# A mixed trunk step on one core: another order of the background work in layer 0

## The chip, the core and the metric

The kernel runs on one core of a Trainium2 chip. A core has TensorE (PE in the profile; its weight loads are PEld), VectorE (DVE), ScalarE (ACT), GpSimd (POOL) and SyncE (SP), which issues most DMAs. Each engine takes its instructions in the order of the program and stops at one whose inputs or buffer aren't there. The metric is device time in microseconds (us). Of the kernel before there are three runs: median 2731.98, from 2730.38 to 2736.82.

## The reference

One step of a decoder trunk of two layers for 1024 prompt tokens and 64 sampled tokens (8 requests of 8), D = 1024. Both layers have the same frame:

```python
h = x
for layer in range(DEPTH):
    hn = rms_norm(h, norm_mix_g[layer])
    # layer 0: conformer_sb_mixer, layer 1: shortconv_pool_mixer
    h = h + mix
    h = h + swiglu(rms_norm(h, norm_ffn_g[layer]), w_ffn_in[layer], w_ffn_out[layer])
y = rms_norm(h, norm_final_g)
```

The change concerns the mixer of layer 0:

```python
proj = hn @ w_in
a_val, a_gate, q, k, v = jnp.split(proj, ...)              # 512 columns each
glu = a_val * jax.nn.sigmoid(a_gate)
a = causal_depthwise_conv(concat([conv_prev, glu]), conv_w) + conv_b   # 31 taps
a = jax.nn.silu(layer_norm(a, ln_g, ln_b))
b = stick_breaking_attention(q, k_all, v_all, sb_bias, q_pos, k_pos)   # 8 heads x 64
out = concat([a, b]) @ w_out
```

and in the attention, for each head and each block of 128 queries,

```python
z = (q @ k.T) * scale + bias
log_1m = jnp.where(mask, jax.nn.log_sigmoid(-z), 0.0)
after = lax.cumsum(log_1m, axis=3, reverse=True) - log_1m
wgt = jnp.exp(jnp.where(mask, jax.nn.log_sigmoid(z) + after, -jnp.inf))
o = wgt @ v
```

The weight of a key is thus sigmoid(z) times the product of sigmoid(-z) over all later keys, and the kernel computes it so, with a running product in place of the sum of logarithms. For the sampled tokens, k and v of 1024 past positions come from a paged cache.

## The kernel before, in words

**Layout and groups.** Activations lie transposed: 128 channels on the partitions, tokens along the free axis, 8 tiles for D. Tokens are in two groups in layer 0: GA is tokens 0 to 511 (one block of 512 columns), GB is tokens 512 to 1087, prompt and samples (two blocks of 288). Layer 1 takes all tokens as GT.

**The foreground.** The matmuls of the projections are the foreground. Each operand is split into a high part in fp32r and the remainder, and `mm3` (L170) makes three passes of high and low parts. Weights stream in pieces of 128x1024: SP loads a piece into `stage`, ACT copies it to the high part of `hl` (L152), POOL subtracts for the low part (L153); `hl` has three buffers. A *block* is one output of 128 channels: 8 tiles by 3 passes by the group's column blocks, 24 matmuls for GA and 48 for GB. DVE then takes the result out of `acc`, times the tokens' norm factors `rr` (`scaled`, L226), or adds it to `hb` (L230). The order of the program is: projection of GA, projection of GB, output projection and FFN of GA, the same of GB, then layer 1.

**Slots and flows.** Within a block, ahead of its tiles 2, 4 and 6, and once behind it, the foreground calls a slot, and a slot runs one piece of the background: up to the next `yield` of the generator at the head of `flow`. So every `yield` in a generator moves all its later work by one slot, a quarter of a block. What a piece issues stands in the engines' queues between the foreground's instructions. Two flows matter:

- `flow_ab` runs during the projection of GB, and begins in that of GA: `conv_a` (the convolution of GA), `conv_norm(GA)` (layer norm and silu), `attention(GA)`. `drain` at the end of GB's projection issues whatever is left of it.
- `flow_c` runs during GA's output projection and FFN: `attention(GB)`, then `conv_b` (the convolution of GB) and `sample` (attention of the sampled tokens on the paged cache) in turn, then `conv_norm(GB)`.

**The norm of the projection.** The projection starts before the factors of the RMS norm are known: the first two blocks' results are kept unscaled in `raw`. `in_proj(GA, ...)` starts at output 2. In the middle of that block `norm_a` sums the squares over the partitions (PE L194, four matmuls of one column), takes the inverse root on ACT and DVE and lays it on a diagonal (`tmp`, DVE L209); behind the block `norm_b` spreads it over the partitions with one matmul by `ones` (PE L218) and copies it to `rr`. The evacuations `evs` of this and of the raw blocks follow. This block runs no slots. `slot_a` counts its calls: it feeds GB's tokens in (`feed`), then GB's own norm, and each call also runs a piece of the background, which starts to work once GB's factors are there (`phase["start"]`).

**conv_a.** For each of four tiles of 128 channels ACT writes the gated values, with 30 columns ahead, into `ext` (L641; one buffer). DVE adds 26 taps into `acc` in PSUM (L653 the first, L655 the others), two to a slot; the 5 others are products on ACT, which POOL adds into `a2` (L647). L660 joins `acc` and `a2` into `a`, which lies in `aall` (shown as hb in the profile).

**conv_norm.** Sums over channels on POOL and PE, squares on ACT, added on POOL into `ss` (L187), which L194 waits for; then for each tile the product with the factors (POOL), the sigmoid of the affine value (ACT), the affine value itself (DVE L744) and the product of both (POOL).

**attention.** A unit is a head and a block of 128 queries, 32 units to a group, four to a head. `s1` computes scores into `z` in PSUM (PE L796) and two sigmoids of it into `q` and `be` (ACT L801); `s2` makes on DVE the running product over `q` by scans and multiplies it into `be` (L815); `s3` turns `be` by PE (L825) into `m` and copies it to `wt` (ACT L826); `s4` multiplies by the values, `o` (PE L834), which ACT copies out (L835). `operands` sets a head's keys and queries up (`kt`, `qa`, `qz`, L773 to L779). In a step u of the loop these run for different units: s4 of u-3, s2 of u-1, for GB a yield, s1 of u, s3 of u-2, then a yield. `zp` and `op_` hold one buffer of z and of o each, `wt` one, `q` two, `be` three.

Of the kernel before, what the change touches and what calls it, by code (L numbers as in the profile page):

```python
# [8 lines left out]
F = mybir.dt.float32  # L9
FR = mybir.dt.float32r  # L10
I32 = mybir.dt.int32
AF = mybir.ActivationFunctionType
OP = mybir.AluOpType
# [45 lines left out]
def trunk_kernel(ctx, tc, x_prompt, x_sample, cache_k, cache_v, state_conformer, state_shortconv, state_pool,  # L59
# [36 lines left out]
    def pc(c):  # L96
        return par[:, c:c + 1]
# [123 lines left out]
    def norm_b(g, ps, dg):  # L221
        spread(g, ps, dg, 1.0)
# [406 lines left out]
    OFF = 5  # L629

    def conv_a(ep, cp):
        g = GA
        for c in range(4):
            while (g.c0, c) not in glu_done:
                yield None
            a = aall[:, c, g.cs]
            ext = ep.tile([128, CW - 1 + HALF], F, name="ext")
            a2 = ep.tile([128, HALF], F, name="a2")
            acc = cp.tile([128, 512], F, name="cacc")
            pool.memset(ext[:, 0:CW - 1], 0.0)  # L640
            act.activation(ext[:, CW - 1:], a, AF.Copy)  # L641

            def otap(j):
                t = a2 if j == 0 else ep.tile([128, HALF], F, name="tapb", bufs=2)
                act.activation(t, ext[:, j:j + HALF], AF.Copy, scale=pc(CONVW + j * 4 + c))
                if j:
                    pool.tensor_tensor(a2, a2, t, op=OP.add)  # L647

            yield 1
            for j in range(OFF, CW):  # L650
                w, i = pc(CONVW + j * 4 + c), ext[:, j:j + HALF]
                if j == OFF:
                    dve.tensor_scalar(acc, i, w, pc(CONVB + c), op0=OP.mult, op1=OP.add)  # L653
                else:
                    dve.scalar_tensor_tensor(acc, i, w, acc, op0=OP.mult, op1=OP.add)  # L655
                if j % 4 == 1 and j // 4 <= OFF:
                    otap(j // 4 - 1)
                if (j - OFF) % 2 == 1:
                    yield 1
            dve.tensor_tensor(a, acc, a2, op=OP.add)  # L660

    def conv_b(ep, cp):
        stc = {}
# [50 lines left out]
    def conv_norm(g):  # L714
# [22 lines left out]
        for c in range(5):  # L737
            if c < 4:
                pool.tensor_tensor(aall[:, c, cs], aall[:, c, cs], rr[:, cs], op=OP.mult)
            if c:  # L740
                y = aall[:, c - 1, cs]
                t = tmp()
                act.activation(t[:, :n], y, AF.Sigmoid, scale=pc(LNG + c - 1), bias=pc(LNB + c - 1))
                dve.tensor_scalar(y, y, pc(LNG + c - 1), pc(LNB + c - 1), op0=OP.mult, op1=OP.add)  # L744
                pool.tensor_tensor(y, y, t[:, :n], op=OP.mult)
            yield 1
            if g is GB:
                yield 1


    def attention(g):
# [3 lines left out]
        with ExitStack() as es_:  # L755
# [31 lines left out]
            def s1(u):  # L787
# [8 lines left out]
                        pe.matmul(z[:, b, :nm], q[:, (i - i0) * 128:(i - i0) * 128 + 128], kt_[h][:, b * w:b * w + nm],  # L796
                                  start=s == 0, stop=s == 1)
                q = qt[u] = pa.tile([128, NKEY], F, name="q2", bufs=2)
                be = bt[u] = pa.tile([128, NKEY], F, name="be", bufs=3)
                for o, sgn, bi in ((q, -0.125, 1), (be, 0.125, 0)):  # L800
                    act.activation(o[:, :n].rearrange("p (b w) -> p b w", b=nb), z[:, 0:nb, :w], AF.Sigmoid,  # L801
                                   scale=sgn, bias=bh[:, bi, h:h + 1])
# [35 lines left out]
            operands(0)  # L838
            while small:
                small.pop(0)()  # L840
            yield 1
            for u in range(len(units) + 3):
                if u >= 3:
                    s4(u - 3)
                if 1 <= u < len(units) + 1:
                    s2(u - 1)
                if g is GB:
                    yield 1
                if u < len(units):
# [3 lines left out]
                    if r == 2 and h < 7:  # L853
                        load_v(h + 1)
                    s1(u)
                if 2 <= u < len(units) + 2:
                    s3(u - 2)
                for _ in range(2):
                    if small:
                        small.pop(0)()  # L860
# [215 lines left out]
    def in_proj(g, x, first, slot):  # L1076
        evs = [(ev_av, ev_ag, ev_q, ev_k, ev_v)[j](g, c) for j, c in EVEN]
        for i in range(first, len(evs)):
            h = w_next()
            a = accs()  # L1080
            if i == first and first:
                box = {}
                block(g, a, h, x, mid=lambda: box.setdefault("d", norm_a(g, ms, D)))
                norm_b(g, ms, box["d"])
                evs[i](a)
                for j in range(2):
                    evs[j](None, raw[j])
# [376 lines left out]
```

## Time and profile before

| | us |
|---|---|
| median of three runs | 2731.98 |
| the profiled execution | 2730.78 |
| its span, first to last instruction | 2729.0 |
| PE busy in the span | 2612.9 |
| DVE, POOL, ACT busy | 1224.5, 1035.5, 860.4 |

The mean granted clock of TensorE is 0.985. The stretch that the change concerns ends at about 1120 us. The projection of GA fills it up to 166, that of GB up to 370, GA's output projection and FFN take the rest: the attention of GB up to 606, the second convolution with the sampled tokens up to 1020, the norm behind it up to 1120. Here, for each stretch, are its length, the busy time of PE, of its weight loads, of DVE, ACT and POOL (with the number of instructions), the granted clock, the busy share of the DMA engines and their GB/s:

```profile
160.00:240.00 80.00, 69.43 (x486) 67.51 (x486) 39.91 (x57) 28.96 (x41) 55.73 (x37) 0.93 0.27 75
240.00:370.00 130.00, 126.35 (x857) 111.20 (x857) 85.91 (x122) 84.03 (x188) 32.07 (x46) 0.97 0.28 78
370.00:606.00 236.00, 214.89 (x1216) 173.88 (x1217) 179.76 (x164) 144.95 (x230) 88.29 (x71) 0.99 0.20 56
1020.00:1120.00 100.00, 83.99 (x337) 64.91 (x337) 38.09 (x54) 32.41 (x45) 67.45 (x39) 0.91 0.31 98
```

A line of a waits view reads "engine, tile, line <- engine, tile, line: us in total, times, longest": the instructions of the left line stood idle until the right one was done. A line of a timeline reads start, duration, engine, line, operation, output<-inputs, shape; "[5.14 <-DVE tmp L209]" is the idle time just ahead and what ended it, and "x8" stands for so many in a row.

### The profile page before, as it was taken

To read this page: it belongs to the slowest core of one execution; us is meant where nothing else is said; L and a number is where in the kernel's file an instruction comes from. 1 tells how busy PE (TensorE), PEld (TensorE's weight loads), DVE (VectorE), ACT (ScalarE), POOL (GpSimd) and SP (SyncE) were. 2 spreads that over 40 slices of the span, in tenths; PEclk is the share of its full clock that TensorE was granted. 3 is DMA by queue.
4 is the path that set the end of the run, shared out by engine and by line. 5 is a ranking of instruction groups with operands and counts; after the bars stand their busy time and mean duration, and the time that the engine had idled before them with its cause. 6 is when DMAs were issued, how large, how long until landed. Compare 5 with 4: busy or idle time off the path is not lost. (4 is left out here: it accounts for less than half of the span.)

```text
span 2729.0 us, 37771 instructions
## 1 busy us (share of the span) xinstructions
PE 2612.9 (96%) x15423; PEld 2370.5 (87%) x15423; DVE 1224.5 (45%) x1738; ACT 860.4 (32%) x1318; POOL 1035.5 (38%) x589
## 2 busy tenths in 40 slices
PE   7988999899999998899999999999999999999997
PEld 5787877777766656899999989999999999999997
DVE  3775767768777652332222243342222222222226
ACT  4435656653343323242222232123211111111112
POOL 5655233433333327454444452223322222222222
PEclk9999999999999998999999999999999999999999
DMA  6332241124445432422222231131111111111111
GB/s 199 108 102 62 60 114 47 54 64 147 133 132 148 125 116 62 151 78 86 79 85 85 86 99 39 39 100 51 46 44 47 47 40 46 47 43 43 47 39 66
DMA packets 293381, 218.75 MB, mean 80 GB/s; under 512 B 21506, under 2 KB 248962, under 8 KB 293193
## 3 DMA queue, kind: packets, MB, share of 16 engines
q1 hardware_dynamic: 293176, 216.33, 26.6%
q8 instruction: 122, 2.00, 0.3%
q14 instruction: 51, 0.41, 0.0%
q10 hardware_dynamic: 32, 0.01, 0.0%
HBM read 198.09 MB, written 18.69 MB: 79 GB/s over the span
## 5 line engine op out<-in xcount | busy, mean ns | idle before, releaser
L153 POOL TENSOR_TENSOR hl<-stage,hl 128x1024 fp32r<-128x1024 f32 x278 | 683.5, 2461 | 1204.6 <-ACT hl L152 790.0
L170 PE MATMUL acc<-x1t,hl 128*128 128x364 f32 (+1 forms) x4896 | 824.1, 330 | 7.1 <-DVE hb L230 6.4
L170 PEld LDWEIGHTS acc<-x1t,hl 128*128 128x128 f32 x4896 | 817.1, 189 | 9.2 <-ACT x1t L304 6.7
L170 PE MATMUL acc<-x,hl 128*128 128x288 f32 (+1 forms) x4704 | 809.3, 326 | 8.8 <-POOL hl L153 3.2
L170 PEld LDWEIGHTS acc<-x,hl 128*128 128x128 f32 x4704 | 688.2, 189 | 88.8 <-issue 36.0
L170 PE MATMUL acc<-hid,hl 128*128 128x364 f32 (+2 forms) x3024 | 534.5, 335 | 19.9 <-DVE hb L230 15.5
L170 PEld LDWEIGHTS acc<-hid,hl 128*128 128x128 f32 x3024 | 482.2, 191 | 58.5 <-DVE hb L230 20.9
L152 ACT ACTIVATE hl<-stage 128x1024 fp32r<-128x1024 f32 x278 | 291.9, 1053 | 584.3 <-PE acc L170 303.1
L226 DVE TENSOR_TENSOR tmp<-acc,rr 128x728 f32<-128x728 f32 (+2 forms) x230 | 160.8, 721 | 698.1 <-PE acc L170 697.2
L230 DVE TENSOR_TENSOR hb<-acc,hb 128x728 f32<-128x728 f32 (+2 forms) x368 | 255.6, 720 | 280.3 <-PE acc L170 278.9
L176 DVE TENSOR_TENSOR hid<-tmp,hid 128x512 fp32r<-128x512 f32 (+2 forms) x66 | 60.8, 921 | 200.7 <-ACT hid L175 200.7
L187 POOL TENSOR_TENSOR ss<-ss,tmp 128x512 f32<-128x512 f32 (+2 forms) x55 | 97.6, 1774 | 92.9 <-ACT tmp L186 91.9
L175 ACT ACTIVATE hid<-tmp 128x512 fp32r<-128x512 f32 (+2 forms) x66 | 53.5, 810 | 238.4 <-POOL tmp L378 238.3
L378 POOL TENSOR_TENSOR tmp<-tmp 128x512 f32<-128x512 f32 (+2 forms) x66 | 117.0, 1772 | 28.0 <-ACT tmp L366 27.9
L170 PE MATMUL acc<-x1a,hl 128*128 128x512 f32 x480 | 123.0, 410 | 3.4 <-POOL hl L153 2.3
L366 ACT ACTIVATE tmp<-tmp 128x576 f32<-128x576 f32 (+1 forms) x44 | 39.6, 900 | 256.1 <-DVE tmp L226 256.1
L170 PEld LDWEIGHTS acc<-x1a,hl 128*128 128x128 f32 x480 | 90.7, 193 | 27.2 <-POOL hl L153 3.8
L834 PE MATMUL o<-wt,vrow 128*64 128x128 f32 x576 | 78.1, 282 | 16.6 <-ACT wt L826 16.6
L834 PEld LDWEIGHTS o<-wt,vrow 128*64 128x64 f32 x576 | 62.5, 139 | 35.5 <-ACT wt L826 30.3
L688 DVE SCALAR_TENSOR_TENSOR cacc<-ext,par,cacc 128x512 f32<-128x512 f32 x120 | 90.1, 750 | 2.3
L364 POOL TENSOR_TENSOR tmp<-tmp 128x512 f32<-128x512 f32 x22 | 32.4, 1471 | 135.9 <-ACT tmp L363 125.1
L813 DVE TENSOR_TENSOR_SCAN q<-q,ones 128x384 f32<-128x384 f32 (+6 forms) x56 | 77.7, 1388 | 2.0
(222 smaller groups left out, 1898.0 us busy)
## 6 DMA issues: line engine op xcount, KB each, us to landing
stage<-in_w_ffn_in_dram SPq DMA_DIRECT2D x132, 512.0 KB
stage<-in_w_ffn_out_dram SPq DMA_DIRECT2D x66, 512.0 KB
stage<-in_w_in_even_dram SPq DMA_DIRECT2D x40, 512.0 KB
kst<-in_cache_k_dram SPq DMA_DIRECT2D x64, 256.0 KB
vst<-in_cache_v_dram SPq DMA_DIRECT2D x64, 256.0 KB
stage<-in_w_out_even_dram SPq DMA_DIRECT2D x16, 512.0 KB
stage<-in_w_in_odd_dram SPq DMA_DIRECT2D x16, 512.0 KB
park<-hb SPq DMA_DIRECT2D x16, 288.0 KB
```

What stands on the lines that cost most here:

```text
L152: act.activation(hl[:, 0], st, AF.Copy)
L153: pool.tensor_tensor(hl[:, 1], st, f32(hl[:, 0]), op=OP.subtract)
L170: pe.matmul(acc[:, b, :c1 - c0], w, x[:, xi, c0:c1], start=first and s == 0, stop=last and s == 2)
L175: act.activation(dst[:, 0], src, AF.Copy)
L176: dve.tensor_tensor(dst[:, 1], src, f32(dst[:, 0]), op=OP.subtract)
L187: pool.tensor_tensor(ss[:, g.cs], ss[:, g.cs], t[:, :g.n], op=OP.add)
L226: dve.tensor_tensor(d, a, r, op=OP.mult)
L230: dve.tensor_tensor(d, a, d, op=OP.add)
L378: pool.tensor_tensor(t[:, :n], t[:, :n], u[:, :n], op=OP.mult)
L688: dve.scalar_tensor_tensor(o, i, w, o, op0=OP.mult, op1=OP.add)
L813: dve.tensor_tensor_scan(e, e, ones[:, 0:1].to_broadcast([128, n - 128]), q[:, n - 128:n - 127], op0=OP.mult, op1=OP.mult)
L834: pe.matmul(o, vrow[h][:, j], w[:, j], start=j == 0, stop=j == i)
```

## The change

Five edits, all in layer 0:

1. `in_proj` for GA: the first of its blocks is held back unevacuated (`held_back`, `acc` has three buffers here), a second block follows, also without slots, and only then come `norm_b` and the evacuations.
2. `conv_a`: the join of a tile's sums is put off to between the taps 7 and 8 of the next tile, or, for the last tile, two yields later. `a2` and `acc` get two buffers; `ext` keeps one.
3. `conv_norm`, both groups: the affine value is computed by ACT (Identity with scale and bias) in place of DVE.
4. `attention`, both groups: three yields in place of one behind the first operands; `s3` directly behind `s4`, ahead of `s2` and `s1`.
5. `be` has two buffers in place of three.

The lines behind move: s1's scores are L801, the sigmoids L806, the last product of `s2` L820, transposes L830, the copy L831, o L839 and its copy L840; the join is L662.

```diff
--- before.py
+++ after.py
@@ -629,14 +629,14 @@
     OFF = 5
 
     def conv_a(ep, cp):
-        g = GA
+        g, last = GA, []
         for c in range(4):
             while (g.c0, c) not in glu_done:
                 yield None
             a = aall[:, c, g.cs]
             ext = ep.tile([128, CW - 1 + HALF], F, name="ext")
-            a2 = ep.tile([128, HALF], F, name="a2")
-            acc = cp.tile([128, 512], F, name="cacc")
+            a2 = ep.tile([128, HALF], F, name="a2", bufs=2)
+            acc = cp.tile([128, 512], F, name="cacc", bufs=2)
             pool.memset(ext[:, 0:CW - 1], 0.0)
             act.activation(ext[:, CW - 1:], a, AF.Copy)
 
@@ -653,11 +653,16 @@
                     dve.tensor_scalar(acc, i, w, pc(CONVB + c), op0=OP.mult, op1=OP.add)
                 else:
                     dve.scalar_tensor_tensor(acc, i, w, acc, op0=OP.mult, op1=OP.add)
+                if j == OFF + 7 and last:
+                    last.pop()()
                 if j % 4 == 1 and j // 4 <= OFF:
                     otap(j // 4 - 1)
                 if (j - OFF) % 2 == 1:
                     yield 1
-            dve.tensor_tensor(a, acc, a2, op=OP.add)
+            last.append(lambda a=a, acc=acc, a2=a2: dve.tensor_tensor(a, acc, a2, op=OP.add))
+        yield 1
+        yield 1
+        last.pop()()
 
     def conv_b(ep, cp):
         stc = {}
@@ -741,7 +746,7 @@
                 y = aall[:, c - 1, cs]
                 t = tmp()
                 act.activation(t[:, :n], y, AF.Sigmoid, scale=pc(LNG + c - 1), bias=pc(LNB + c - 1))
-                dve.tensor_scalar(y, y, pc(LNG + c - 1), pc(LNB + c - 1), op0=OP.mult, op1=OP.add)
+                act.activation(y, y, AF.Identity, scale=pc(LNG + c - 1), bias=pc(LNB + c - 1))
                 pool.tensor_tensor(y, y, t[:, :n], op=OP.mult)
             yield 1
             if g is GB:
@@ -796,7 +801,7 @@
                         pe.matmul(z[:, b, :nm], q[:, (i - i0) * 128:(i - i0) * 128 + 128], kt_[h][:, b * w:b * w + nm],
                                   start=s == 0, stop=s == 1)
                 q = qt[u] = pa.tile([128, NKEY], F, name="q2", bufs=2)
-                be = bt[u] = pa.tile([128, NKEY], F, name="be", bufs=3)
+                be = bt[u] = pa.tile([128, NKEY], F, name="be", bufs=2)
                 for o, sgn, bi in ((q, -0.125, 1), (be, 0.125, 0)):
                     act.activation(o[:, :n].rearrange("p (b w) -> p b w", b=nb), z[:, 0:nb, :w], AF.Sigmoid,
                                    scale=sgn, bias=bh[:, bi, h:h + 1])
@@ -838,10 +843,13 @@
             operands(0)
             while small:
                 small.pop(0)()
-            yield 1
+            for _ in range(3):
+                yield 1
             for u in range(len(units) + 3):
                 if u >= 3:
                     s4(u - 3)
+                if 2 <= u < len(units) + 2:
+                    s3(u - 2)
                 if 1 <= u < len(units) + 1:
                     s2(u - 1)
                 if g is GB:
@@ -853,8 +861,6 @@
                     if r == 2 and h < 7:
                         load_v(h + 1)
                     s1(u)
-                if 2 <= u < len(units) + 2:
-                    s3(u - 2)
                 for _ in range(2):
                     if small:
                         small.pop(0)()
@@ -1081,7 +1087,12 @@
             if i == first and first:
                 box = {}
                 block(g, a, h, x, mid=lambda: box.setdefault("d", norm_a(g, ms, D)))
+                held_back = a
+                continue
+            elif i == first + 1 and first:
+                block(g, a, h, x)
                 norm_b(g, ms, box["d"])
+                evs[first](held_back)
                 evs[i](a)
                 for j in range(2):
                     evs[j](None, raw[j])
```

How the order of instructions changes at three places. First PE, in the projection of GA, as a piece of the difference: `x1a` are the eight tiles of GA's input, three passes to each row, so eight rows are a block; L218 spreads the norm factors.

```order
 L170 MATMUL acc<-x1a_117,hl 128x512 x3
 L170 MATMUL acc<-x1a_118,hl 128x512 x3
+L170 MATMUL acc<-x1a_111,hl 128x512 x3
+L170 MATMUL acc<-x1a_112,hl 128x512 x3
+L170 MATMUL acc<-x1a_113,hl 128x512 x3
+L170 MATMUL acc<-x1a_114,hl 128x512 x3
+L170 MATMUL acc<-x1a_115,hl 128x512 x3
+L170 MATMUL acc<-x1a_116,hl 128x512 x3
+L170 MATMUL acc<-x1a_117,hl 128x512 x3
+L170 MATMUL acc<-x1a_118,hl 128x512 x3
 L218 MATMUL m<-tmp,ones 128x512
```

One more block stands ahead of the spreading matmul.

Second DVE, in the last third of GA's projection: taps (L653, L655), products of the projection (L226, with `tmp` for values of v) and joins. Before:

```order
L655 SCALAR_TENSOR_TENSOR cacc<-ext,par,cacc 128x512 x8
L226 TENSOR_TENSOR tmp<-acc,rr 128x512
L660 TENSOR_TENSOR hb<-cacc,a_983 128x512
L653 TENSOR_SCALAR cacc<-ext,par 128x512
L655 SCALAR_TENSOR_TENSOR cacc<-ext,par,cacc 128x512 x5
L226 TENSOR_TENSOR tmp<-acc,rr 128x512
L655 SCALAR_TENSOR_TENSOR cacc<-ext,par,cacc 128x512 x8
L226 TENSOR_TENSOR tmp<-acc,rr 128x512
L655 SCALAR_TENSOR_TENSOR cacc<-ext,par,cacc 128x512 x8
L226 TENSOR_TENSOR tmp<-acc,rr 128x512
```

and now:

```order
L655 SCALAR_TENSOR_TENSOR cacc<-ext,par,cacc 128x512 x8
L226 TENSOR_TENSOR tmp<-acc,rr 128x512
L653 TENSOR_SCALAR cacc<-ext,par 128x512
L655 SCALAR_TENSOR_TENSOR cacc<-ext,par,cacc 128x512 x5
L226 TENSOR_TENSOR tmp<-acc,rr 128x512
L655 SCALAR_TENSOR_TENSOR cacc<-ext,par,cacc 128x512 x2
L662 TENSOR_TENSOR hb<-cacc,a_1016 128x512
L655 SCALAR_TENSOR_TENSOR cacc<-ext,par,cacc 128x512 x6
L226 TENSOR_TENSOR tmp<-acc,rr 128x512
L655 SCALAR_TENSOR_TENSOR cacc<-ext,par,cacc 128x512 x8
L226 TENSOR_TENSOR tmp<-acc,rr 128x576
```

The join L660, now L662, no longer stands between the last tap of a tile and the first of the next; eight taps stand between two products as before. The last rows of each are the last product of GA; behind the new order's row of 128x512 stands GB's first, of 576 columns.

Third ACT, within a unit of GB's attention in the FFN of GA. L835 (now L840) copies o out, L826 (now L831) copies the turned weights, L801 (now L806) are the sigmoids, L152 is a piece of the streamed weights. Before:

```order
L835 ACTIVATE hb<-o_4445 64x128
L152 ACTIVATE hl<-stage 128x1024
L801 ACTIVATE q_4473<-z_4468,bh 128x896
L801 ACTIVATE be<-z_4468,bh 128x896
L826 ACTIVATE wt<-m 128x512
L826 ACTIVATE wt<-m 128x128
```

and now:

```order
L840 ACTIVATE hb<-o_4408 64x128
L831 ACTIVATE wt<-m 128x512
L831 ACTIVATE wt<-m 128x256
L152 ACTIVATE hl<-stage 128x1024
L806 ACTIVATE q_4450<-z_4445,bh 128x1024
L806 ACTIVATE be<-z_4445,bh 128x1024
```

The copies of a unit's turned weights stand directly behind the copy of o and ahead of the sigmoids; before, they stood behind them. On PE the transposes stand accordingly: behind o of the unit before, ahead of the scores.

## The prediction

> **What bounds the kernel now.** I read the page, then who waited for whom on PE, then the granted clock by stretch, then the four engines' order of time in each stretch with waits. In the page's busy line, PE (TensorE) has work in 96% of the span, so it is the bound wherever it isn't held up.
>
> ```profile
> span 2729.0 us, 37771 instructions
> PE 2612.9 (96%) x15423; PEld 2370.5 (87%) x15423; DVE 1224.5 (45%) x1738; ACT 860.4 (32%) x1318; POOL 1035.5 (38%) x589
> ```
>
> The change adds no matmul and takes none, so only PE's idle time and the slow clock behind it can move. The waits on PE, each with its total in us, the times and the longest:
>
> ```profile
> PE o L834 <- ACT wt L826: 16.6, 18, 3.5
> PE m L601 <- DVE tmp L226: 7.3, 3, 6.2
> ...
> PE m L218 <- DVE tmp L209: 5.1, 1, 5.1
> PE z L796 <- ACT qa L778: 3.8, 1, 3.8
> PE z L796 <- POOL qz L762: 2.3, 1, 2.3
> PE m L194 <- POOL ss L187: 2.2, 1, 2.2
> PE z L796 <- DVE kt L776: 1.5, 1, 1.5
> PE z L796 <- DVE qz L779: 0.8, 1, 0.8
> ```
>
> These are places that the change touches: o waits for copied attention weights, m at L601 for the last value product, m at L218 for the norm factors, z for the operands of the first scores. Behind the longer ones the granted clock (the number ahead of the DMA share, third from the end) stands at 0.50:
>
> ```profile
> 39.80:46.50 6.70, 4.56 (x9) 2.98 (x10) 3.64 (x11) 0.60 (x1) 0.00 (x0) 0.50 0.33 89
> 159.30:166.00 6.70, 4.34 (x19) 4.37 (x20) 5.76 (x9) 2.17 (x3) 1.55 (x1) 0.50 0.34 93
> 217.30:220.60 3.30, 3.30 (x16) 3.30 (x15) 1.19 (x4) 0.00 (x0) 0.00 (x0) 0.50 0.54 158
> 237.80:244.50 6.70, 4.56 (x17) 4.50 (x18) 4.81 (x5) 2.65 (x5) 2.59 (x4) 0.50 0.48 119
> 486.90:490.20 3.30, 3.23 (x15) 2.90 (x15) 3.30 (x2) 0.40 (x2) 3.30 (x2) 0.50 0.39 113
> ```
>
> Work in such a stretch takes twice as long, so half of what PE does there is lost as well.
>
> **The change part by part.**
>
> *A, norm factors and the end of group A's projection.* PE comes to L218 too early:
>
> ```profile
> 41.94 2.05 PE L218 MATMUL m<-tmp,ones 128*128 128x512 f32 x2 [5.14 <-DVE tmp L209]
> 80.37 5.86 PE L170 MATMUL acc<-x1a,hl 128*128 128x512 f32 x24
> ```
>
> The last row is one block of this group, 24 matmuls: 5.86. One block more ahead of L218 covers the 5.14 and leaves 0.7 over. The half clock goes with it: from 41.94 to 46.5 PE works at half speed, which loses 4.6 / 2 = 2.3. That is 7.4 at this place. But no background slot runs during that block, and its four slots are lost to the work behind, so the convolution starts a block later in the program: in time 7.4 - 5.9 = 1.5 us earlier than today. From there DVE (VectorE) sets the pace:
>
> ```profile
> 100.00:150.00 50.00, 48.47 (x216) 38.38 (x215) 47.95 (x67) 20.59 (x29) 32.33 (x21) 1.00 0.35 100
> 154.63 6.29 DVE L655 SCALAR_TENSOR_TENSOR cacc<-ext,par,cacc 128x512 f32<-128x512 f32 x8
> 160.82 0.69 DVE L226 TENSOR_TENSOR tmp<-acc,rr 128x512 f32<-128x512 f32 x1
> 161.66 1.09 PE L601 MATMUL m<-ident,tmp 128*128 128x128 f32 x4 [6.17 <-DVE tmp L226]
> 118.38 0.64 ACT L641 ACTIVATE ext<-hb 128x512 f32<-128x512 f32 x1 [5.11 <-DVE cacc L655]
> 118.39 0.69 DVE L660 TENSOR_TENSOR hb<-cacc,a 128x512 f32<-128x512 f32 x1
> 119.22 0.81 DVE L653 TENSOR_SCALAR cacc<-ext,par 128x512 f32<-128x512 f32 x1
> ```
>
> DVE is busy for 47.95 of these 50 us. A block brings it eight taps (6.29) and one product (0.69), 7.0 for PE's 5.86, so it falls behind, and at the end PE waits for the last value product, which is done at 161.5. That end is a sum of DVE's own work, and I move it term by term: it starts 1.5 earlier; in the new order 66 taps stand between the first tap and this product where 74 stood, -6.3; one product fewer, -0.6. Joining the sums late takes no wait away: L660 starts as the taps end, so a2 was there. But the join fills the time in which ScalarE rewrites ext, of which there is still one buffer (taps end 118.3, ext 118.38 to 119.02, next tap 119.22). With the join gone from there, that time lies bare twice, some 0.65 more each, +1.3. Together -7.1: the product ends at 154.4, and since PE itself comes 7.4 earlier and meets no wait at L218, it waits at L601 for about 7 as today, with the half clock behind it. I take 7.0 for both edits together; bounds 5 (each ext costs a whole write more) and 10 (the end's own wait shrinks by its half clock and more). The taps that now fall into group B meet blocks of 6.6 us (48 matmuls, below) with two buffers, 7.0 of DVE for 6.6: five such blocks let it fall 2 us behind, which a buffer covers, so they cost nothing; without that cover it would be those 2.
>
> *B, conv norm of group A.* L194 waits 2.2 for POOL's last sum of squares. In the new order one product of the GLU stands ahead of the norm's work there instead of within it, some 1.3 us (POOL's rate for 512 columns, L153's 2.79 halved), so the wait falls under 1; with the half clock of the row 217.30 (3.3 / 2) up to 3.9 go. I take 2.5, bounds -1 and 3.9. The affine on ScalarE costs about what a 512-wide write costs it (ext, 0.64) four times, where VectorE's took the same, in the same chain of sigmoid, affine and product: nothing by itself. Without the cover of POOL's products it would be 4 x 0.64.
>
> The Trainium skill (TensorE: Matmul & The Clock Gate, section "What's actually happening") has the clock fall to half after at least one idle window of about 3.4 us; by that the wait of 2.17 would cost no clock and the sum would be 1.7 smaller; the row 217.30 shows 0.50 behind it, so the trace differs, and the sum keeps it.
>
> *C, first scores of group A.* Three yields for one are two slots more, 24 of a block's 48 matmuls, 3.3 us:
>
> ```profile
> 236.46 2.79 POOL L153 TENSOR_TENSOR hl<-stage,hl 128x1024 fp32r<-128x1024 f32 x1
> 239.31 1.09 POOL L762 MEMSET qz<- 64x512 f32 x2
> 346.57 6.62 PE L170 MATMUL acc<-x,hl 128*128 128x288 f32 x48
> ```
>
> Of the 3.8 and 2.3 the slots cover 3.3. The clears of qz now stand ahead of the weight subtract (2.8 less), but the four affines come ahead of qa on ScalarE (4 x 0.64, that is 2.6 more, partly beside POOL's products). I leave 2.7 of wait: 3.4, and about half of what the half clock costs PE there (4.5 / 2), in all 4.6; bounds 1 and 8.4.
>
> *E, first scores of group B:* 1.5 + 0.8 = 2.3, and two slots are 12 matmuls of 512 columns there, half of 5.86; I take 2.3, bounds 1 and 2.3.
>
> *D and F, copied weights.* Of the 16.6 in 18 waits, 15.6 lie in group B between 371 and 606, with 3.3 / 2 = 1.7 of clock at 487, and 1.0 in group A, of which I take 0.8 (D), bounds 0 and 1. Group B:
>
> ```profile
> 555.20 0.77 ACT L826 ACTIVATE wt<-m 128x512 f32<-128x512 f32 x2
> 555.85 1.31 PE L834 MATMUL o<-wt,vrow 128*64 128x128 f32 x10 [2.31 <-ACT wt L826]
> 550.18 0.69 DVE L176 TENSOR_TENSOR hid<-tmp,hid 128x512 fp32r<-128x512 f32 x1 [5.54 <-ACT hid L175]
> 510.78 0.96 DVE L815 TENSOR_TENSOR be<-be,q 128x767 f32<-128x767 f32 x1
> 537.90 3.35 POOL L153 TENSOR_TENSOR hl<-stage,hl 128x1024 fp32r<-128x1024 f32 x1 [3.82 <-ACT hl L152]
> 539.18 2.89 DVE L815 TENSOR_TENSOR be<-be,q 128x767 f32<-128x767 f32 x1
> 540.72 1.74 PE L834 MATMUL o<-wt,vrow 128*64 128x128 f32 x14
> ```
>
> The first two rows: the copy ends at 555.97, behind the sigmoids on ScalarE, and PE has stood for it since 553.5. In the new order transposes and copy come half a unit earlier, right behind the unit before, ahead of the sigmoids, and a whole unit (25 us for a head's four, so about 6.2) lies between them and L834: that wait ends. What is late next is be, since the transposes now follow L834 of the unit before directly. In the last two rows be ended at 542.07 and that L834 at 542.46, a margin of 0.4. In the 400s it is larger:
>
> ```profile
> 445.11 0.82 DVE L815 TENSOR_TENSOR be<-be,q 128x639 f32<-128x639 f32 x1
> 448.23 1.52 PE L834 MATMUL o<-wt,vrow 128*64 128x128 f32 x12 [0.65 <-ACT wt L826]
> 400.00:425.00 25.00, 23.82 (x142) 19.35 (x141) 20.63 (x17) 16.10 (x26) 9.37 (x8) 1.00 0.20 53
> ```
>
> 445.93 against 449.75, so 3.8, with DVE busy for 20.63 of 25. In the FFN part DVE stands idle 5.54 for hid and then works without a break; there a PE that is 1.2 us a head faster or more meets margins of 0.4 and waits for be instead. I leave 4.3 of the 17.3 for this (two heads at about 2, the rest single) and take 13.0. Bounds: 17.3 (nothing waits) and 4 (the margin is gone in every unit). Two be buffers in place of three cost nothing, for the transposes that free one stand ahead of the scores that fill it; with the old order of the two it would be a wait in each unit.
>
> *G, conv norm of group B.* POOL comes to L378, the product of the FFN, late:
>
> ```profile
> 1044.98 1.27 POOL L378 TENSOR_TENSOR tmp<-tmp 128x512 f32<-128x512 f32 x1
> 1048.82 6.58 PE L170 MATMUL acc<-hid,hl 128*128 128x512 f32 x18 [4.50 <-DVE hb L230]
> ```
>
> With the norm two slots later, one of its adds and one weight subtract trade places with this product, about 1.4 + 1.4 less ahead of it, and the affine no longer holds VectorE while ScalarE computes the sigmoid. The last products of this norm end as before, since POOL has the same work there and little idle time. I take 2.5 of the 4.5; bounds -3 (the waits behind it grow as PE comes earlier) and 7 (4.5 and its half clock). Should POOL be later than today, the cast of hid, the adds to hb and then PE are late in turn.
>
> *H:* attention of group B ends two slots later, so the sampled rows and the second convolution move by two slots against the FFN's blocks, with the page loads that SP issues for them. The waits that end there may grow or shrink by this; nothing says which way, so I take 0, and for bounds twice the 2.2 of B either way, -4 and 4. The weights' own loads keep their order and their distance.
>
> Sum: 7.0 + 2.5 + 4.6 + 0.8 + 2.3 + 13.0 + 2.5 = 32.7 us. The profiled execution took 2730.8 (2729.0 span and 1.8 around it), which gives 2698.1; the median of the runs, 2732.0, lies 1.2 above it: **2699**.
>
> **The rivals.**
> *All covers hold:* margins at be suffice, and clock loss goes as well. A 9, B 3.9, C 8.4, D 1, E 2.3, F 17.3, G 7 are 49: 2683. For it: margins of 2 to 5 us in the 400s; against it: DVE's unbroken stretches.
> *VectorE takes over:* be arrives late in nearly each unit. F 4, A 5, C 1, B 1, E 2.3, G 0 are 13: 2719. For it: 2.89 where 0.96 were needed. The Trainium skill (SBUF — State Buffer, section "Who interferes with whom") says that a VectorE instruction with two SBUF inputs and a GpSimd one that reads SBUF exclude each other for the whole of the first; the rows 537.90 and 539.18 agree.
> *The ScalarE queue blocks, slower:* each unit's weight copies now stand at the head, and behind them the sigmoids, the hid cast and the weight split hl. If be is late by over 2 us in a unit, all of it stops, and the next scores with it. At 2.5 us for each of 32 units of group B that is 80, less the 20 of the other items: 2791. It decides where a head brings VectorE more than its 25 us; the row 400.00 shows 20.63, so this is unlikely.
> *Given back:* DVE or POOL sets where a group ends, as in A, at the other ends too; then the waits only move, 2730.
>
> **How the numbers follow.** Forecast 0.54 (own range 2688 to 2710, by the bounds of F, C and H), all covers 0.15, VectorE 0.2, given back 0.06, blocked queue 0.05. Range 2679 to 2722, which takes in the first two rivals. What a measurement can tell here is about 0.3%, 8 us. Faster: 0.54 + 0.15 + 0.18 = 0.87 (VectorE's case can fall short by 5 us, hence 0.02 of it); the same 0.02 + 0.05 = 0.07; slower 0.05 + 0.01 = 0.06.
>
> **What would show it.** A: no wait at L218 and 6 to 8 us still at the last L601. B: under 1 at L194. C: 1 to 3 at the first scores. F: hardly any wait of o on wt, 3 to 6 us of transposes on DVE be. G: 1 to 3 us at the wait on hb of 4.5. I am wrong if the waits on be sum to over 10, or if the L601 wait goes, since then DVE did not set group A's end.

## The result and the profile after

The changed kernel takes 2708.73 us (four runs, 2706.65 to 2710.94), the kernel before 2731.18 beside it: ratio 0.9914, 95% interval 0.9896 to 0.9931. It is faster by 22.4 us. The forecast was 2699, so 32 were expected and 10 of them are missing.

The page of the changed kernel, the span and the busy line. PE does the same 15423 matmuls in a span 22.2 us shorter:

```profile
span 2706.8 us, 37823 instructions
PE 2603.3 (96%) x15423; PEld 2365.3 (87%) x15423; DVE 1212.3 (45%) x1730; ACT 868.3 (32%) x1326; POOL 1031.1 (38%) x589
```

Who PE waits for, in the changed kernel (total, times, longest):

```profile
PE acc L170 <- DVE hb L230: 33.6, 10, 7.4
PE m L1000 <- ACT wts L1001: 9.5, 4, 3.7
PE m L830 <- DVE be L820: 9.5, 7, 3.5
PE m L601 <- DVE tmp L226: 6.7, 2, 6.2
...
PE z L801 <- ACT crow L588: 3.2, 1, 3.2
...
PE m L218 <- DVE tmp L209: 0.8, 2, 0.7
...
PE o L839 <- ACT wt L831: 0.4, 1, 0.4
```

Read against the rows before: the wait at L218 went from 5.1 to 0.8, that at L194 left the list, the first scores went from 6.1 in two waits to 3.2 in one, and the waits of o on the copied weights from 16.6 to 0.4. The last L601 still waits 6.2. Three rows grew. The transposes now wait for be (9.5). The other two read, in the kernel before:

```profile
PE acc L170 <- DVE hb L230: 24.2, 9, 6.4
PE m L994 <- ACT wts L995: 6.4, 4, 2.5
```

L1000, then L994, belongs to the sampled tokens; other waits of that line fell from 3.6 to 0.5, so with them it waits 10.0 in both kernels. The row of L230, which the prediction left alone but for one wait of 4.5, holds a new wait of 7.4.

That new wait stands at the end of group A's output projection. The timeline of the changed kernel there, on PE, DVE and POOL:

```profile
445.91 8.87 PE L170 MATMUL acc<-x,hl 128*128 128x512 f32 x27 [7.38 <-DVE hb L230]
439.50 5.55 DVE L781 TENSOR_TENSOR kt<-kall,kt 64x512 fp32r<-64x512 f32 x2
445.07 1.29 DVE L230 TENSOR_TENSOR hb<-acc,hb 128x512 f32<-128x512 f32 x2
439.41 5.09 POOL L153 TENSOR_TENSOR hl<-stage,hl 128x1024 fp32r<-128x1024 f32 x2 [0.86 <-ACT hl L152]
```

and its busy time by stretch behind the wait, with the granted clock third from the end:

```profile
440.90:451.00 10.10, 5.09 (x12) 4.05 (x13) 8.38 (x6) 3.66 (x5) 6.49 (x4) 0.50 0.35 104
```

and of the kernel before, the same work:

```profile
455.75 1.29 DVE L776 TENSOR_TENSOR kt<-kall,kt 64x512 fp32r<-64x512 f32 x2
461.71 1.27 DVE L230 TENSOR_TENSOR hb<-acc,hb 128x512 f32<-128x512 f32 x2
460.02 0.10 POOL L803 MEMSET be<- 128x1 f32 x1 [5.78 <-ACT be L801]
462.74 5.17 POOL L153 TENSOR_TENSOR hl<-stage,hl 128x1024 fp32r<-128x1024 f32 x2 [2.62 <-ACT hl L152]
462.72 0.74 PE L170 MATMUL acc<-x,hl 128*128 128x512 f32 x2 [1.50 <-ACT hl L152]
465.16 6.10 PE L170 MATMUL acc<-x,hl 128*128 128x512 f32 x25 [1.71 <-POOL hl L153]
```

The two key splits of a head took 1.29 before, with POOL idle, and 5.55 after, where POOL's two weight splits had begun 0.09 us ahead of them. The last results of the projection, L230, stand behind the key splits on DVE, and the FFN on PE stands behind those. With the half clock (5.09 busy at half speed, 2.5 lost) the place costs 9.9; before, it cost 3.2, the two waits on hl at 462.7 and 465.2. Clock and wait together are thus 6.7 worse than before at this one place.

### The profile page after: what moved, and what is told of

Read it like the earlier page. It is cut to its first block, busy times and chain, and to the rows that moved or that the text cites. A ratio compares the mean times of both kernels' runs of the same rounds, so it can differ in the third digit from the quotient of the medians.

```text
span 2706.8 us, 37823 instructions
## 1 busy us (share of the span) xinstructions
PE 2603.3 (96%) x15423; PEld 2365.3 (87%) x15423; DVE 1212.3 (45%) x1730; ACT 868.3 (32%) x1326; POOL 1031.1 (38%) x589
## 5 line engine op out<-in xcount | busy, mean ns | idle before, releaser
L152 ACT ACTIVATE hl<-stage 128x1024 fp32r<-128x1024 f32 x278 | 292.1, 1054 | 585.9 <-PE acc L170 318.5
L226 DVE TENSOR_TENSOR tmp<-acc,rr 128x728 f32<-128x728 f32 (+2 forms) x230 | 160.6, 720 | 684.3 <-PE acc L170 681.6
L230 DVE TENSOR_TENSOR hb<-acc,hb 128x728 f32<-128x728 f32 (+2 forms) x368 | 255.3, 720 | 273.2 <-PE acc L170 272.2
L693 DVE SCALAR_TENSOR_TENSOR cacc<-ext,par,cacc 128x512 f32<-128x512 f32 x120 | 90.1, 751 | 2.3
L839 PE MATMUL o<-wt,vrow 128*64 128x128 f32 x576 | 76.6, 278 | 0.4 <-ACT wt L831 0.4
L655 DVE SCALAR_TENSOR_TENSOR cacc<-ext,par,cacc 128x512 f32<-128x512 f32 x100 | 75.4, 754 | 3.0
```

Source lines behind the costliest of these rows:

```text
L152: act.activation(hl[:, 0], st, AF.Copy)
L226: dve.tensor_tensor(d, a, r, op=OP.mult)
L230: dve.tensor_tensor(d, a, d, op=OP.add)
L693: dve.scalar_tensor_tensor(o, i, w, o, op0=OP.mult, op1=OP.add)
L839: pe.matmul(o, vrow[h][:, j], w[:, j], start=j == 0, stop=j == i)
```

## The experiments

Each is the changed kernel (2708.7) with one thing altered, until a better version becomes the base.

**One yield for group B (gb_yield1).** Is the collision due to the two added slots?

```diff
-            for _ in range(3):
+            for _ in range(3 if g is GA else 1):
                 yield 1
```

> The changed kernel, but the attention of group B has one yield behind its first operands, as before the change; group A keeps three. Theory (collision): the two extra slots bring the key splits of one head (DVE L781, 5.55 us for two at 439.5) beside the two weight splits that close group A's output projection (POOL L153, 5.09 us at 439.4), so that the results of that projection (DVE L230) come late and PE waits 7.4 us with 10.2 us of half clock behind it, 12.5 us in all, where the kernel before lost 3.2. Without the two slots that wait is under 3, some 9 us come back, less about 2 at the first scores of group B that the slots cover: 2708.7 - 7 = 2702, between 2699 and 2705. Rival (order): the wait comes from the new order of transposes and products, whatever the slots; then it stays at 5 or more and the time is 2709 to 2712.

Measured: 2712.37 (2711.09 to 2713.64). The timeline of this kernel:

```profile
439.48 1.29 DVE L781 TENSOR_TENSOR kt<-kall,kt 64x512 fp32r<-64x512 f32 x2
446.25 0.70 PE L170 MATMUL acc<-x,hl 128*128 128x512 f32 x2 [2.06 <-DVE hb L230]
358.08 0.48 PE L801 MATMUL z<-kt,qa 128*128 128x512 f32 x1 [2.83 <-DVE kt L781]
```

The collision is gone, as the theory had it: 1.29 again, and a wait of 2.06. The time is not: it rose by 3.6. At the first scores of group B a wait of 2.8 came up that the two slots cover, and behind the place of the collision the transposes waited 8.6 for be in place of 5.1. But over the whole span PE stood idle for 100.5 us, less than the 103.5 of the changed kernel; what grew is the loss by half clock, from 22.1 to 30.6 (half of what PE does in the stretches at 0.50, counted from the two traces), and 8.8 more are lost behind the attention of group B, where the waits are 3.3 shorter. Moving all of a flow by two slots removes one meeting and changes much else; the expected 2702 had counted the collision and the first scores alone. Whether the moved slots or the place of the clock's stretches made the later loss, no run separates.

**The turned weights in their old place (old_order).**

```diff
                 if u >= 3:
                     s4(u - 3)
-                if 2 <= u < len(units) + 2:
-                    s3(u - 2)
...
                     s1(u)
+                if 2 <= u < len(units) + 2:
+                    s3(u - 2)
```

with three buffers of be.

> The changed kernel with the turned weights in their old place (s3 behind s1) and three be buffers, both groups; all else as changed. Theory (collision): the wait on DVE L230 at the end of group A's output projection stays at 6 to 8 us, since the slots are as in the changed kernel. The waits of o on the copied weights come back with about 15 us and the waits of the transposes on be (9.5) go: 2708.7 + 6 = 2715, between 2711 and 2720. Rival (order): the wait on L230 shrinks below 3, and the time is 2708 or less.

Measured: 2712.64 (2711.52 to 2713.29). The waits of this kernel between 357 and 592:

```profile
PE o L839 <- ACT wt L831: 15.2, 15, 3.9
PE acc L170 <- DVE hb L230: 2.5, 1, 2.5
```

and its timeline where the two splits meet:

```profile
441.67 1.29 DVE L781 TENSOR_TENSOR kt<-kall,kt 64x512 fp32r<-64x512 f32 x2
442.34 5.63 POOL L153 TENSOR_TENSOR hl<-stage,hl 128x1024 fp32r<-128x1024 f32 x2 [1.52 <-ACT hl L152]
```

Both theories failed in part. The slots are those of the changed kernel, yet there is no collision: in the old order the copy of wt stands on ScalarE between the sigmoids and the weight copies, POOL starts 0.67 us behind DVE instead of 0.09 ahead of it, and the key splits pass. So it takes both edits, the slots and the order. And the order is worth only 3.9 in this company, because undoing it also undoes the collision.

**The norm factors a block earlier (norm_early)**, with the late joins kept:

```diff
-                held_back = a
-                continue
-            elif i == first + 1 and first:
-                block(g, a, h, x)
                 norm_b(g, ms, box["d"])
-                evs[first](held_back)
                 evs[i](a)
```

> The changed kernel with the norm factors spread behind the first block of in_proj(GA) again, as before the change; the late joins and all else stay. Theory (the held block carries item A): the wait at L218 is back with 5.1 us and 6.8 us of half clock, the last L601 ends at about 162, and the whole is 6 to 7 us slower: 2715, between 2713 and 2718. Rival (the late joins carry it): the end of group A's projection stays within 2 us of the changed kernel's 157, and the time is 2709 to 2711.

Measured: 2720.38 (2716.56 to 2723.33), 11.7 slower; two runs lie at 2717 and 2718, two at 2723, and the profiled one is the slowest. The timeline of this kernel on PE:

```profile
43.67 2.05 PE L218 MATMUL m<-tmp,ones 128*128 128x512 f32 x2 [4.82 <-DVE tmp L209]
163.98 1.09 PE L601 MATMUL m<-ident,tmp 128*128 128x128 f32 x4 [6.17 <-DVE tmp L226]
219.29 1.67 PE L194 MATMUL m<-ones,ss 128*128 128x1 f32 x8 [1.87 <-POOL ss L187]
```

The first two rows are item A: the wait of 4.8 is back, and the last L601 starts 7.7 us later than in the changed kernel (163.98 against 156.28) with the same wait of 6.2 ahead of it. The third is more than was expected: the wait at L194 is back too, so item B hangs on the block that is held back, and not on the affine.

**The operands one unit later (kt_late)**, in group B only:

```diff
-                    if r == 0 and h < 7:
+                    if r == (1 if g is GB else 0) and h < 7:
                         operands(h + 1)
```

> The changed kernel, but in group B the operands of the next head are queued one unit later (at its second unit instead of its first), so that the key splits on DVE fall one unit later and not beside the weight splits at the end of group A's output projection; the slots stay as changed. Theory (collision): the wait on DVE L230 there falls below 4, and the time by 4 to 10 us, unless the splits meet other heads' work later: 2702, between 2698 and 2707. Rival (order): the wait stays above 5, and the time within 2 us of 2708.7.

Measured: 2705.37 (2705.02 to 2706.09), 3.4 less than the changed kernel. On PE:

```profile
440.22 1.22 PE L170 MATMUL acc<-x,hl 128*128 128x512 f32 x2 [2.30 <-ACT hl L152]
442.67 3.78 PE L170 MATMUL acc<-x,hl 128*128 128x512 f32 x8 [1.23 <-POOL hl L153]
```

The wait on DVE is gone with the key splits; what is late next is the weight itself, whose copy stands on ScalarE behind the head's first two operand copies (1.67).

**The operands two units later (kt_late2)**, three to a unit, so that these copies too leave the place:

```diff
-                    if r == 0 and h < 7:
+                    if r == (2 if g is GB else 0) and h < 7:
...
-                for _ in range(2):
+                for _ in range(3 if g is GB else 2):
                     if small:
```

> The changed kernel, but in group B the operands of the next head are queued at its third unit and issued three to a unit, so that neither their copies on ScalarE (L778, 1.05 and 0.62) nor the key splits on DVE stand ahead of the weight pieces that close group A's output projection. Theory: in the run with the operands one unit later the wait there was still 2.3 on the copy of the weights and 1.2 on their split, behind those copies; without them it falls to about 2 in all with at most 3.4 us of half clock: 2705.4 - 3 = 2702, between 2699 and 2706. Rival: the operands then meet the start of the FFN, the first scores of a head wait for qz, and the time is above 2707.

Measured: 2700.98 (2700.80 to 2702.24); against the kernel before 0.9885, interval 0.9868 to 0.9901. On PE:

```profile
437.73 0.73 PE L170 MATMUL acc<-x,hl 128*128 128x512 f32 x2 [0.85 <-ACT hl L152]
440.17 6.01 PE L170 MATMUL acc<-x,hl 128*128 128x512 f32 x18 [1.71 <-POOL hl L153]
```

2.6 of waiting in place of 7.4, and 7.7 us less than the changed kernel, with every part of the change kept: the collision and its clock are what the changed kernel lost.

**The same with the turned weights in their old place (kt_late2_old)**: what is the order worth without the collision? The edit is that of the second experiment, on this base.

> The kernel with the operands queued two units later, and the turned weights in their old place (s3 behind s1) with three be buffers. Theory: the new order by itself is worth what the copied weights made o wait, less the waits on be: in the run old_order the former were 15.3 us and some 4 of half clock, in kt_late2 the latter are 7.5 with 3.4; so this kernel takes 2701 + 9 = 2710, between 2707 and 2714, where the same undoing cost the changed kernel only 3.9, because it also undid the collision. Rival (the order is worth no more than those 3.9): 2703 to 2706.

Measured: 2712.81 (2711.38 to 2713.53), 11.8 above its base. The waits between 357 and 592 of this kernel, then of its base between 357 and 585:

```profile
PE o L839 <- ACT wt L831: 14.7, 15, 3.9
```

```profile
PE m L830 <- DVE be L820: 5.8, 3, 3.5
...
PE o L839 <- ACT wt L831: 0.4, 1, 0.4
```

14.7 of waiting for copies turn into 5.8 for be, in three places. By the medians the order is worth 11.8 without the collision, three times what the second experiment showed. Not all of it is shown to be the order's own work: the two profiled spans differ by 10.3, of which 6.4 are idle time and half clock within the attention of group B (1.6 in the second experiment), while 3.3 arise behind it, as half clock behind waits that are alike.

**The joins early (join_early), the affine on DVE (affine_dve), one yield for group A (ga_yield1)**: three undoings of one edit each.

```diff
-                if j == OFF + 7 and last:
-                    last.pop()()
...
-            last.append(lambda a=a, acc=acc, a2=a2: dve.tensor_tensor(a, acc, a2, op=OP.add))
+            dve.tensor_tensor(a, acc, a2, op=OP.add)
```

> The changed kernel with each tile's sums joined right behind its last tap again (both two-buffer tiles and the two last yields stay). Theory: the late join takes no wait away, it only left the rewriting of ext bare: 2708.7 - 0.5, between 2706.5 and 2710, and the wait at the last L601 between 5.2 and 6.3. Rival (the join waits for the sums of ScalarE and POOL in a2): DVE stands before each join, the end of group A's projection is 2 us later or more, and the time above 2711.

```diff
-                act.activation(y, y, AF.Identity, scale=pc(LNG + c - 1), bias=pc(LNB + c - 1))
+                dve.tensor_scalar(y, y, pc(LNG + c - 1), pc(LNB + c - 1), op0=OP.mult, op1=OP.add)
```

> The changed kernel with the affine value of both conv norms on DVE again. Theory: it is worth nothing by itself: 2708.7 within 2; the wait at L194 stays gone, since that hangs on the block held back, not on the affine; the first scores of group A wait up to 2 us less than 3.2, as four writes of 0.8 us leave ScalarE's queue ahead of qa. Rival (VectorE was held up by the affine): the waits behind conv norm of group B between 1010 and 1100 grow by 2 us or more, and the time is 2711 to 2714.

```diff
-            for _ in range(3):
+            for _ in range(1 if g is GA else 3):
                 yield 1
```

> The changed kernel with one yield behind the first operands of group A's attention (group B keeps three). Theory: the two slots cover 3.3 us of waiting for the operands; the wait at the first scores grows from 3.2 to about 6.5, and the half clock behind it from 3.4 to 6.8 us: 2708.7 + 5 = 2714, between 2712 and 2716. Rival (what the slots cover is given back where the flow is drained at the end of group B's projection): within 1.5 of 2708.7.

Measured: 2708.41 (2707.28 to 2710.06) and 2708.59 (2706.70 to 2710.42), neither to be told from the changed kernel, and 2712.10 (2709.80 to 2713.18), 3.4 slower. In the last one PE waits 6.3 at the first scores in place of 3.2, as expected, and the half clock behind it is 6.8 us long; with the affine on DVE these scores wait 2.45 and 0.95, no less than the 3.2 of the changed kernel, so the 2 us that I had allowed there were not to be had.

**No taps ahead of the last value product (quiet_last).** Does DVE set the end of group A?

```diff
-                block(g, a, h, x, slot=slot)
+                quiet = first and i == len(evs) - 1
+                block(g, a, h, x, slot=skip if quiet else slot)
                 flush()
                 evs[i](a)
-            slot()
+            if first and i == len(evs) - 2:
+                skip()
+            else:
+                slot()
...
+    def skip():
+        turn[0] += 1
...
-                if (j - OFF) % 2 == 1:
+                if (j - OFF) % 2 == 1 if c < 3 or j < OFF + 8 else (j - OFF) % 3 == 2:
                     yield 1
```

> The kernel with the operands queued two units later, and no slots within and just ahead of the last block of group A's projection, so that eight taps less stand ahead of the last value product on DVE; in group B the last tile's later taps come three to a slot, so that the flow ends one slot later. Theory (DVE sets the end of group A): the wait at the last L601 falls from 6.2 to about 1, the half clock behind it goes, and one drained slot costs up to 1: 2701 - 6.5 = 2694.5, between 2692 and 2698. Rival 1 (PE's wait there has another cause): the wait stays above 4, 2700 to 2703. Rival 2 (given back): DVE falls behind in group B, with 9.1 us of taps to a block of 6.6, and new waits on its products bring it to 2698 to 2703.

Measured: 2701.36 (2700.78 to 2702.18), no gain on its base of 2700.98. The timeline of DVE and PE at the end of group A:

```profile
148.81 0.69 DVE L226 TENSOR_TENSOR tmp<-acc,rr 128x512 f32<-128x512 f32 x1 [0.82 <-PE acc L170]
149.65 0.63 PE L601 MATMUL m<-ident,tmp 128*128 128x128 f32 x4 [0.44 <-DVE tmp L226]
```

and this kernel's waits between 220 and 340:

```profile
PE m L830 <- DVE be L820: 6.4, 8, 1.2
PE z L801 <- DVE kt L781: 4.2, 1, 4.2
```

DVE did set the end: with the taps out of the way it waits for PE (0.82) and PE's wait falls from 6.2 to 0.4. The 8 us are lost again by 350: where the base waits 2.2 for be and 3.2 at the first scores in this stretch, this kernel waits 6.4 and 4.2, half clock costs it 2.7 more, and its flow is drained one slot longer. That was the price of rival 2, though not by its mechanism: DVE did not hold PE up while it worked off the taps.

**The same, one slot earlier behind the convolution (quiet_phase).**

```diff
-        yield 1
         yield 1
         last.pop()()
```

> The run before with one yield instead of two ahead of the last tile's join, so that conv norm and attention of group A stand in the same slots against group B's blocks as in kt_late2, and only the taps are moved. Theory (in quiet_last the 8.4 us won at the end of group A were lost again because the attention of group A stood one slot further on, so that its products of be met other work on DVE and it was drained one slot longer): the end of group A stays 8 us early and the stretches behind it are those of kt_late2, give or take 1.5: 2701 - 7.5 = 2693.5, between 2690 and 2697. Rival (the chain of conv norm and attention of group A bounds that stretch, whatever the foreground does): the waits behind grow by what was won, and the time is 2698 to 2703.

Measured: 2694.50 (2693.51 to 2694.86); against the kernel before 0.9860, interval 0.9844 to 0.9877. It is faster than both kernels of this study. Its waits between 215 and 335 are those of kt_late2 again:

```profile
PE z L800 <- ACT crow L588: 3.2, 1, 3.2
PE m L829 <- DVE be L819: 1.7, 2, 1.1
```

One slot of position, with the same work, made 6.9 us.

## Why the prediction was right, and where it was wrong

The single undoings, against the changed kernel:

| undone | us | more |
|---|---|---|
| norm factors a block later | 2720.4 | 11.7 |
| two more yields, group A | 2712.1 | 3.4 |
| two more yields, group B | 2712.4 | 3.6 |
| turned weights ahead | 2712.6 | 3.9 |
| late join | 2708.4 | -0.3 |
| affine on ScalarE | 2708.6 | -0.1 |

They sum to 22.2, about the whole gain, but not because the parts are independent: the price of the order depends on its company, as shown above. Nor is a row the waits of its edit alone. With the yields of group A, those of group B or the order undone, PE stands idle for 103.9, 100.5 and 102.0 us in the profiled execution, hardly more or even less than the 103.5 of the changed kernel; what they lose more of is clock, 26.2, 30.6 and 26.0 in place of 22.1.

- **A (7.0) and B (2.5): right, B too small.** The last product ended at 156.1 where 154.4 was worked out. The profiled execution was already 1.75 late ahead of all that the change touches (its first L194 starts at 34.69, before at 32.94), so the sum came out as worked out; PE waited 6.2 where about 7 were said. The step that holds the sum up, that DVE sets this end and that the late join takes no wait away, is shown by norm_early, join_early and quiet_last. B was worth its upper bound: the wait of 2.2 and its half clock, 3.9, went together. Undoing the held block costs 11.7, against 9.5 for both, in runs that lie up to 6.8 apart.
- **C (4.6): right.** 6.1 of waiting became 3.2, where 2.7 were left; ga_yield1 puts the two slots at 3.4. **D (0.8) was wrong in sign:** in group A the waits on be came to 1.9, where the waits on copies had been 1.0.
- **E (2.3): right in kind.** Undoing the yields of group B brings back 2.8 of wait at the first scores where 0.8 stand now, with half clock behind it.
- **F (13.0): this is the step that failed.** Its mechanism was right: the waits of o are gone, be is late next, the two longest of its waits (3.5 and 2.0) stand beside POOL's weight splits, and between 357 and 590 they sum to 7.5, where 4.3 were left for them. Its size was too large even without the collision: for E and F together 15.3 were forecast, and in kt_late2 idle time and half clock in the attention of group B are 8.7 below the kernel before; be waits longer than was left for it, and half clock costs 4.5 there where it cost 1.8. In the changed kernel only 1.0 of it is left. What the step did not look at is what stands behind DVE's other work of the same flow. I compared be with the L834 ahead of it and stopped there. The key splits moved as well, by the two slots and by the order of ScalarE, and met POOL's weight splits; the results of the projection behind them, not be, were late. I had the rows: 537.90 and 539.18 show such a meeting, and I priced it for be alone. It cost the 7.7 us that kt_late2 wins back, most of the 10 that are missing.
- **G (2.5) and H (0):** the waits on L230 and L226 between 1020 and 1120, 15.8 before, are 15.9 in the changed kernel's same stretch (13.8 + 2.1); two new waits, on POOL, add 1.9, and half clock costs 2.7 less, so that the stretch gained 0.9. The affine, which G counted in part, did nothing. G was too large by about its whole size in waiting. Between 606 and 1020, H's place, 2.1 went, more than half of it clock.
- **The rivals.** The queue of ScalarE did not block. "VectorE takes over" described what PE waits for better than its 2719 suggests: be in seven places, and DVE once more in L230. The measured 2708.7 lies halfway between the forecast and this rival. The forecast's own range was summed too tightly: the bounds of F, C and H, added, give 2687 to 2716, not 2688 to 2710.
- The sign by which I would have been wrong, waits on be over 10, was nearly met (9.5); the other, that the wait at L601 goes, was not.

Counted from the two traces, idle time and half clock fell by 7.0 up to the end of group A's projection (A), by 4.4 from there to the first scores of group A (B), by 3.7 up to the attention of group B (C and D), by 1.0 in that attention (E and F) and by 2.6 behind it, 18.7 in all.

Not settled: the span fell by 22.2. The other 3.4 lie in what PE does at full clock, and no run took them apart.

## What to carry to other kernels

When background work is moved by a slot or two, list what else of it moves, on every engine, and look at the few places where the foreground has a deadline: an operand split on DVE that meets a weight split on POOL there costs four times its length, and everything behind it on DVE is late. An edit's worth, found by undoing it, holds in that company only: the same order was worth 3.9 beside the collision and 11.8 without it, and where an undoing makes 3 or 4 us, look whether PE waited more or was only granted less clock. A place that is bound by DVE, not by a wait, is mended by taking DVE's work away from it, and the win is kept only if what follows keeps its position.

## What the runs showed of the hardware

**Who comes first decides.** DVE's two key splits took 1.29 when they began 0.67 ahead of POOL's weight splits, and 5.55 when they began 0.09 behind. The Trainium skill (SBUF — State Buffer, section "Who interferes with whom") says so: issue order decides who blocks, for the whole of the instruction; the rows agree, and show how little it takes. The convolution's taps, which read one operand from PSUM, kept their 0.75 beside POOL's work. The same meeting at the start of the FFN, in the changed kernel's timeline:

```profile
469.16 3.05 DVE L820 TENSOR_TENSOR be<-be,q 128x895 f32<-128x895 f32 x1
468.36 6.07 POOL L153 TENSOR_TENSOR hl<-stage,hl 128x1024 fp32r<-128x1024 f32 x2 [2.81 <-ACT hl L152]
472.36 1.73 PE L830 MATMUL m<-ident,be 128*128 128x128 f32 x7 [3.49 <-DVE be L820]
```

and its granted clock behind it:

```profile
471.60:478.30 6.70, 5.94 (x19) 5.26 (x20) 6.22 (x5) 1.64 (x4) 2.87 (x2) 0.50 0.67 185
```

**The same wait does not always cost clock.** In the run with the affine on DVE the same wait of 3.49 is followed by full clock; in the changed kernel half clock stands there for 6.7 us, in which PE works 5.9 and loses 3. The timeline of the run with the affine on DVE:

```profile
474.49 0.95 PE L830 MATMUL m<-ident,be 128*128 128x128 f32 x7 [3.49 <-DVE be L820]
```

and its stretch behind the wait, at 1.00:

```profile
473.00:480.00 7.00, 5.51 (x34) 4.73 (x35) 6.83 (x5) 3.20 (x6) 3.72 (x4) 1.00 0.55 153
```

What made the difference can be read from the clock records. In each of the thirteen traces of this case the half-clock stretches begin on a grid of 3.41 us, and what counts is how long PE was idle within the window of that grid just ahead. Between 25 and 2690 us, all 126 windows at full clock with more than 2.0 us of idle time were followed by half clock; of 9699 with less than 1.6, one was (1.17, in the kernel before at 213.8); of the 64 between, 29 were. In the changed kernel one window held 2.66 of idle time; with the affine on DVE the grid cut the wait into 2.0 and 1.5, and full clock went on.

So a sum that adds half the clock stretch to each wait is an average, and two kernels that wait alike can differ by some us for this alone.
